# The place of weight splits in the tails of a two-layer hybrid decoder: ahead of the whole layer norm instead of its last 30 instructions

## The chip, the cores and the metric

The kernel runs on one core of one Trainium2 chip. The metric is device time in microseconds (us) of one execution; below is the better. TensorE (PE) multiplies, VectorE (DVE) and ScalarE (ACT) do the elementwise work, GpSimd (POOL) a few additions, and SyncE (SP) starts the transfers. Each engine takes its instructions in the order in which the program lists them.

## What is computed

The input x has 512 positions of 1024 channels. Layer 0 is a mixer of a short convolution and a gated DeltaNet, layer 1 an HGRN2 recurrence; both end in an output projection. What follows each mixer is the tail, and the tails are what this change is about:

```python
for i in range(DEPTH):
    s = conv_gdn_mixer(...) if i % 2 == 0 else hgrn2_mixer(...)      # its last step: y @ w_out
    x = layer_norm(DEEPNORM_ALPHA * x + s, ln_g[i], ln_b[i])
    gate = jax.nn.sigmoid((x @ w_pl_gate[i]).astype(jnp.float32))
    x = x + ((p[i] @ w_pl[i]).astype(jnp.float32) * gate).astype(x.dtype)
```

Everything is float32. A product of two float32 operands is made of three products on TensorE: each operand is split into a high part in a shorter format and the rest, and high x high, low x high and high x low are added (lines 115 to 117).

## The kernel before, in words

All data lie channel by channel: 128 channels on the partitions, 512 positions along them, so that x is eight tiles `f` of 128 x 512. Weights come in chunks of 128 x 1024 float32 (0.5 MB). For each chunk SP starts the load into `wraw` (line 105), ScalarE casts it into `whi` (line 107) and VectorE subtracts the two into `wlo` (line 108). All three have three buffers. So the cast of a chunk waits until TensorE is done with the chunk three before, and a load waits until the split of the chunk three before is done. Accumulators in PSUM for projections are also three (line 70): a fourth takes the first one's buffer and waits until that has been read.

`tail` (line 911) is called twice, for the even and the odd layer. In order:

- `out_proj` (line 923) multiplies the mixer's output with the chunks of the output weight into `pout`; VectorE adds the scaled residual while it reads the result out into `rr` (line 941), and GpSimd sums the eight tiles into `racc` (line 945). Tiles 0 to 3 are done for all 512 positions, tiles 4 to 7 in two halves of 256 positions (`hf` 0 and 1). In the second half tile 4 is the last.
- `norm_half` (line 962) normalizes a half: the mean `mu` as a matmul with a constant (line 966), VectorE subtracts it from the eight tiles (line 971), ScalarE squares (line 973), VectorE adds up into `qacc` (line 975), the variance `var` by a matmul (line 977), then `ve` (line 979) and three Newton steps for the inverse square root (lines 155 to 159), each of three instructions that need the one before, the product with it (line 983), scale and offset on ScalarE (line 985), and the split of the result into `x1h` and `x1l` (lines 163 and 164). The first half's norm runs beside the second half's output projection, the second half's beside what follows.
- The projection of p, `ppl`: two chunks of w_pl, eight tiles of six matmuls of 512 columns each; ScalarE scales each into `pl` (line 1014).
- The gate, `pgate`: eight chunks of w_pl_gate, eight tiles f, each half 24 matmuls of 256 columns. The first halves of tiles 0, 1 and 2 come first, then, when the second norm is done, their second halves, then the other tiles. Tanh on ScalarE (line 1026), two steps on VectorE (lines 1027 and 1028), and a store.

A scheduler puts the instructions of each engine into order by their priority, which falls along the program as it is written; `norm_half` is fed in between the matmuls of the other work by a list of steps (`pump`, line 125). An offset lifts instructions above those written up to so many places earlier:

```python
with self.tc.high_priority(offset=self.prio):
    nc.scalar.copy(hi, raw)
    nc.vector.tensor_tensor(lo, raw, hi.bitcast(F32), op=SUB)
```

`self.prio` is 0 in the layers. The tail sets it to `PRIO` (line 42) at line 992, ahead of the second halves of the output projection, and back to 0 at its end.

Of the kernel before, what the change touches and what calls it, by code (L numbers as in the profile page):

```python
# [38 lines left out]
LN = 2, 7  # L39
GD = 7, 4, 4, 9, 4, 3  # L40
EO = 'f0 g f1 a0 f2 a1 f3 a2 f4 a3 f5 a4 f6 f7 a5 a6 a7'
PRIO = 30


SM_CA, SM_CB, SM_AL, SM_DT, SM_GN, SM_HN, SM_LN, SM_LB, SM_N = 0, 24, 120, 128, 136, 137, 138, 170, 202
# [2 lines left out]
class K:  # L48
# [862 lines left out]
    def tail(self, layer, wout, last):  # L911
# [5 lines left out]
        with tp(name=f"tail{layer}", bufs=1, reuse_waits="tile") as lp, self.psum(f"pt{layer}") as self.ps:  # L917
# [5 lines left out]
            def out_proj(fs, t0, n, held=None):  # L923

                ts = slice(t0, t0 + n)
                accs = [self.acc("pout")[:, :n] for _ in fs]
                chunks = list(held or [])
                for i in range(2):
                    kh = 1 - i if held else i
                    for j, (f, ps) in enumerate(zip(fs, accs)):  # L930
                        if not held or i:
                            chunks.append(self.chunk(wout[2 * f + kh], 16 if n == S else 32))
                        hi, lo = chunks[-1 if not held or i else j]
                        for k in range(8):
                            self.mm3(ps, [(hi[:, k, :], lo[:, k, :], self.yh[kh * 8 + k][:, ts],
                                           self.yl[kh * 8 + k][:, ts])], i == 0 and k == 0, i == 1 and k == 7)
                            self.pump(n / S)
                for f, ps in zip(fs, accs):
                    xr = lp.tile([P, S], F32, tag="xr", name="xr", bufs=2)[:, :n]
                    nc.sync.dma_start(xr, xsrc[:, f * S + t0:f * S + t0 + n])  # L940
                    nc.vector.scalar_tensor_tensor(rr[f][:, ts], xr, ALPHA, ps, op0=MUL, op1=ADD)
                    for hf in range(t0 // HT, (t0 + n) // HT):
                        hs = slice(hf * HT, (hf + 1) * HT)
                        if f:
                            nc.gpsimd.tensor_tensor(racc[hf], rr[0][:, hs] if f == 1 else racc[hf],
                                                    rr[f][:, hs], op=ADD)
                return chunks[-len(fs):]
# [5 lines left out]
            def load_p():  # L953
                praw = self.wp.tile([P, 2 * S], F32, tag="wraw", name="praw", bufs=3)
                nc.sync.dma_start(praw, a["pT"][layer])
                self.split_to(ph.rearrange("p a b -> p (a b)"), pl_.rearrange("p a b -> p (a b)"), praw)
# [34 lines left out]
            held = out_proj((5, 6, 7), 0, HT)  # L991
            self.prio = PRIO
            load_p()
# [134 lines left out]
```

## Time and profile before

| | us |
|---|---|
| median of 3 runs (1216.73 to 1220.0) | 1218.28 |
| the profiled execution | 1218.49 |
| its span, first to last instruction | 1216.8 |
| TensorE busy in it | 1198.5 |
| VectorE, ScalarE, GpSimd busy | 805.7, 563.4, 46.1 |

The even tail stands at about 478 to 627 us of the span, the odd one at 1086 us to its end. Times in the rows are us from the start of the span. A timeline row gives start, length, engine, line, operation, what it writes and reads, and in brackets how long the engine was idle before and what ended that. A matmul's length goes from its issue to the modelled end of its passage, so lengths overlap and the distance between starts is the pace. Where equal instructions follow each other, one row gives them all (x4).

### The profile page before, as it was taken

The numbers are of one execution on the slowest core, as the hardware profiler recorded it, in microseconds if no ns is written. First come the engines' busy times: TensorE is split into PE (matmuls) and PEld (weight loads), VectorE is DVE, ScalarE is ACT, GpSimd is POOL, SyncE is SP. The second block draws the span as 40 slices with busy tenths as digits, with TensorE's granted clock in tenths as the row PEclk, the third lists the DMA queues.
The fourth block names the chain that finished last, engine by engine and source line by source line (L and its number), as shares of the span: only waits on it lengthen the run. The fifth ranks groups of instructions, "written<-read, shape, count | busy, mean of one in ns | idle before, by whom it ended". The sixth has DMA issues, their size and how long they took to land.

```text
span 1216.8 us, 23689 instructions
## 1 busy us (share of the span) xinstructions
PE 1198.5 (98%) x9590; PEld 1020.4 (84%) x9590; DVE 805.7 (66%) x1835; ACT 563.4 (46%) x1340; POOL 46.1 (4%) x75
## 2 busy tenths in 40 slices
PE   7999999999999999999999999999999999999998
PEld 5777878777788788898998888888888888889988
DVE  7778767776768755349856575665657575744884
ACT  5554645454545443127633444444544444433471
POOL 4000000000000000111000000000000000001100
PEclk9999999999999999999999999999999999999999
DMA  6223222222223123353442222222122222234422
GB/s 213 91 79 94 69 88 88 70 90 85 87 71 97 61 70 104 126 161 120 141 148 81 77 88 70 88 69 90 53 87 88 70 88 70 88 104 152 143 92 100
DMA packets 37310, 117.08 MB, mean 96 GB/s; under 512 B 4144, under 2 KB 8016, under 8 KB 37200
## 3 DMA queue, kind: packets, MB, share of 16 engines
q1 hardware_dynamic: 37200, 115.56, 29.5%
q8 instruction: 75, 1.23, 0.4%
q14 instruction: 35, 0.29, 0.1%
HBM read 111.32 MB, written 4.23 MB: 95 GB/s over the span
## 4 chain that ended last, share of the span: by engine, by line
PE 84%; DVE 8%; ACT 4%; DMA 1%; issue 1%; POOL 0%; SPq 0%; DVEq 0%; ACTq 0%; POOLq 0%
PE pz L115 5%; PE pz L117 5%; PE pz L116 5%; PE pout L115 4%; PE pout L117 4%; PE pout L116 4%; PE pqkv L116 3%; PE pqkv L117 3%; PE pqkv L115 3%; PE pf L115 3%; PE pf L117 2%; PE pf L116 2%; PE pq L115 2%; PE pq L117 2%; PE pq L116 2%; PE pgate L116 2%
## 5 line engine op out<-in xcount | busy, mean ns | idle before, releaser
L107 ACT CAST whi<-wraw 128x1024 fp32r<-128x1024 f32 (+1 forms) x196 | 200.4, 1022 | 333.1 <-PE pout L116 86.6
L108 DVE TENSOR_TENSOR wlo<-wraw,whi 128x1024 fp32r<-128x1024 f32 (+1 forms) x196 | 238.3, 1216 | 161.7 <-ACT whi L107 156.8
L115 PE MATMUL pout<-yh,whi 128*128 128x256 f32 (+1 forms) x384 | 122.3, 319 | 0.0
L117 PE MATMUL pout<-yh,wlo 128*128 128x256 f32 (+1 forms) x384 | 122.1, 318 | 0.0
L116 PE MATMUL pout<-yl,whi 128*128 128x256 f32 (+1 forms) x384 | 121.7, 317 | 0.0
L115 PE MATMUL pz<-xh,whi 128*128 128x512 f32 x256 | 103.7, 405 | 0.2 <-DVE scr L413 0.2
L117 PE MATMUL pz<-xh,wlo 128*128 128x512 f32 x256 | 100.6, 393 | 0.0
L116 PE MATMUL pz<-xl,whi 128*128 128x512 f32 x256 | 100.3, 392 | 0.0
L115 PE MATMUL pqkv<-xh,whi 128*128 128x512 f32 x192 | 78.9, 411 | 5.0 <-ACT xh L163 5.0
L117 PE MATMUL pqkv<-xh,wlo 128*128 128x512 f32 x192 | 77.2, 402 | 2.3 <-DVE wlo L108 2.3
L116 PE MATMUL pqkv<-xl,whi 128*128 128x512 f32 x192 | 78.0, 406 | 0.0
L116 PEld LDWEIGHTS pout<-yl,whi 128*128 128x128 f32 x384 | 72.9, 190 | 5.0
L115 PEld LDWEIGHTS pout<-yh,whi 128*128 128x128 f32 x384 | 72.2, 188 | 5.1
L117 PEld LDWEIGHTS pout<-yh,wlo 128*128 128x128 f32 x384 | 72.3, 188 | 5.0
L115 PE MATMUL pi<-whi,xh 128*128 128x256 f32 x256 | 72.7, 284 | 0.0
L116 PE MATMUL pi<-wlo,xh 128*128 128x256 f32 x256 | 72.1, 282 | 0.0
L116 PE MATMUL pgate<-x1l,whi 128*128 128x256 f32 x256 | 71.2, 281 | 0.4 <-DVE x1l L164 0.4
L117 PE MATMUL pi<-whi,xl 128*128 128x256 f32 x256 | 71.2, 278 | 0.0
L117 PE MATMUL pgate<-x1h,wlo 128*128 128x256 f32 x256 | 70.8, 279 | 0.0
L115 PE MATMUL pgate<-x1h,whi 128*128 128x256 f32 x256 | 70.7, 281 | 0.0
L117 PEld LDWEIGHTS pz<-xh,wlo 128*128 128x128 f32 x256 | 48.1, 188 | 10.2
L115 PEld LDWEIGHTS pz<-xh,whi 128*128 128x128 f32 x256 | 48.1, 188 | 9.9 <-issue 0.6
(326 smaller groups left out, 2865.5 us busy)
## 6 DMA issues: line engine op xcount, KB each, us to landing
wraw<-in_we SPq DMA_DIRECT2D x62, 512.0 KB, 3.5
wraw<-in_wo SPq DMA_DIRECT2D x48, 512.0 KB, 3.5
wraw<-in_woe SPq DMA_DIRECT2D x21, 512.0 KB, 3.5
wraw<-in_woo SPq DMA_DIRECT2D x21, 512.0 KB, 3.5
wraw<-in_wg SPq DMA_DIRECT2D x16, 512.0 KB, 3.6
wraw<-in_wi SPq DMA_DIRECT2D x16, 512.0 KB, 3.4
gb<-drows SPq DMA_DIRECT2D x8, 512.0 KB, 3.7
xraw<-in_xT SPq DMA_DIRECT2D x8, 256.0 KB, 4.4
```

The costliest lines, as they stand in the source:

```text
L107: nc.scalar.copy(hi, raw)
L108: nc.vector.tensor_tensor(lo, raw, hi.bitcast(F32), op=SUB)
L115: nc.tensor.matmul(ps, wh, xh, start=first and i == 0, stop=False)
L116: nc.tensor.matmul(ps, wh, xl, start=False, stop=False)
L117: nc.tensor.matmul(ps, wl, xh, start=False, stop=last and i == n - 1)
```

## The change

One number is another. The offset of the splits in the tails goes from 30 to 600 places, so that the scheduler puts a split ahead of the whole layer norm, as soon as its place in the program allows, and not only ahead of the 30 instructions that were written before it. Loads, buffers, tiles and arithmetic stay as they are.

```diff
@@ -39,7 +39,7 @@
 LN = 2, 7
 GD = 7, 4, 4, 9, 4, 3
 EO = 'f0 g f1 a0 f2 a1 f3 a2 f4 a3 f5 a4 f6 f7 a5 a6 a7'
-PRIO = 30
+PRIO = 600
```

The same difference appears in both tails. In the names below (the even tail) a number at the end tells tiles of one name apart: `wlo_6302`, `wlo_6345` and `wlo_6375` are splits of the last three chunks of the output weight, `wlo_6429` and `wlo_6506` those of the two chunks of w_pl, `wlo_6595`, `wlo_6626` and `wlo_6657` those of the first three chunks of w_pl_gate. A leading - is the place before, + the place now.

VectorE, at the end of the first half's sums of squares:

```order
+L108 TENSOR_TENSOR wlo_6302<-wraw_6300,whi_6301 128x1024 [waits DMAHW4_49,PE_49,Activation_49]
 L975 TENSOR_TENSOR qacc_6104<-qacc_6104,sq_6129 128x256 [waits DVE_49,Activation_49]
 L975 TENSOR_TENSOR qacc_6104<-qacc_6104,sq_6133 128x256 [waits DVE_49,Activation_49]
-L108 TENSOR_TENSOR wlo_6302<-wraw_6300,whi_6301 128x1024 [waits DMAHW4_49,PE_49,Activation_49]
+L941 SCALAR_TENSOR_TENSOR rr5_5534<-xr_6330,pout_6083 128x256 [waits DMAHW5_49,PE_49]
 L979 TENSOR_SCALAR ve_6179<-var_6103 128x256 [waits PE_49]
+L108 TENSOR_TENSOR wlo_6345<-wraw_6343,whi_6344 128x1024 [waits DMAHW7_49,Activation_49]
```

The split of a chunk now stands ahead of the last two sums, and the next split between `ve` and the inverse square root; the evacuation of tile 5 has come ahead of `ve`.

VectorE, at the end of the first half's norm, around the evacuation of the second half's last tile (`rr4`, from `pout_6342`):

```order
+L108 TENSOR_TENSOR wlo_6595<-wraw_6593,whi_6594 128x1024 [waits DMAHW5_49,PE_49,Activation_49]
 L164 TENSOR_TENSOR x1l0_2_6072<-rr2_5531,x1h0_2_6071 128x256 [waits Activation_49]
 L164 TENSOR_TENSOR x1l0_3_6074<-rr3_5532,x1h0_3_6073 128x256 [waits Activation_49]
 L164 TENSOR_TENSOR x1l0_4_6076<-rr4_5533,x1h0_4_6075 128x256 [waits Activation_49]
+L983 TENSOR_TENSOR rr7_5536<-rr7_5536,lny_6181 128x256 [waits DVE_49]
+L941 SCALAR_TENSOR_TENSOR rr4_5533<-xr_6403,pout_6342 128x256 [waits DMAHW4_49]
 L164 TENSOR_TENSOR x1l0_5_6078<-rr5_5534,x1h0_5_6077 128x256 [waits Activation_49]
-L941 SCALAR_TENSOR_TENSOR rr4_5533<-xr_6403,pout_6342 128x256 [waits DMAHW4_49,PE_49]
```

The split of the first chunk of w_pl_gate was 16 places behind `rr4` and is now five ahead of it; that of the second chunk of w_pl was eight behind and is now 12 ahead, among the products of line 983, and that of the first chunk of w_pl, which stood five ahead, is now inside the Newton steps.

TensorE, in the projection of p; `ppl_6486` is its third tile:

```order
 L116 MATMUL ppl_6442<-pl_5540,whi_6428 128x512
 L117 MATMUL ppl_6442<-ph_5539,wlo_6429 128x512
-L966 MATMUL mu_6449<-racc1_5538,onesD_220 128x256 [waits Pool_49]
 L115 MATMUL ppl_6486<-ph_5539,whi_6428 128x512 [waits DVE_49]
 L116 MATMUL ppl_6486<-pl_5540,whi_6428 128x512
+L966 MATMUL mu_6449<-racc1_5538,onesD_220 128x256 [waits Pool_49]
```

The mean of the second half has gone two matmuls back. The variance of the second half moves on TensorE from behind the ninth gate matmul to behind the first, and on VectorE the split `wlo_6657` from ahead of its `ve` to behind it. After the norm two gate chunks' casts go ahead of the first two tanh. On ScalarE a cast moves with each split.

## Rows read from the trace of the kernel before

**Rows 1.** The page: busy us (share of the span) and instructions of each engine.

```profile
PE 1198.5 (98%) x9590; PEld 1020.4 (84%) x9590; DVE 805.7 (66%) x1835; ACT 563.4 (46%) x1340; POOL 46.1 (4%) x75
```

**Rows 2.** TensorE's waits in the tails: us in total, times, longest.

```profile
PE ppl L117 <- DVE wlo L108: 1.9, 2, 1.2
...
PE pgate L116 <- DVE x1l L164: 0.4, 2, 0.2
```

**Rows 3.** Timeline of TensorE, even tail: start, length, instruction, idle before.

```profile
554.94 0.67 PE L977 MATMUL var<-qacc,onesD 128*128 128x256 f32 x2
...
568.29 0.39 PE L115 MATMUL ppl<-ph,whi 128*128 128x512 f32 x1
...
569.64 0.50 PE L117 MATMUL ppl<-ph,wlo 128*128 128x512 f32 x1 [0.72 <-DVE wlo L108]
...
572.20 0.70 PE L966 MATMUL mu<-racc,onesD 128*128 128x256 f32 x2
...
581.04 0.28 PE L115 MATMUL pgate<-x1h,whi 128*128 128x256 f32 x1
...
590.22 0.29 PE L115 MATMUL pgate<-x1h,whi 128*128 128x256 f32 x1
590.71 0.38 PE L116 MATMUL pgate<-x1l,whi 128*128 128x256 f32 x1 [0.20 <-DVE x1l L164]
```

**Rows 4.** Timeline of TensorE, odd tail.

```profile
1154.06 0.40 PE L115 MATMUL ppl<-ph,whi 128*128 128x512 f32 x1
...
1155.84 0.50 PE L117 MATMUL ppl<-ph,wlo 128*128 128x512 f32 x1 [1.15 <-DVE wlo L108]
...
1176.28 0.39 PE L115 MATMUL pgate<-x1h,whi 128*128 128x256 f32 x1
1176.87 0.39 PE L116 MATMUL pgate<-x1l,whi 128*128 128x256 f32 x1 [0.20 <-DVE x1l L164]
```

**Rows 5.** Busy us of each engine in two stretches, even tail; PEclk, DMA share, GB/s.

```profile
550.00:560.00 10.00, 10.00 (x85) 9.94 (x84) 9.77 (x19) 4.61 (x7) 0.85 (x1) 1.00 0.53 161
560.00:570.00 10.00, 9.28 (x76) 8.79 (x75) 9.87 (x22) 6.63 (x14) 1.57 (x2) 1.00 0.39 130
```

**Rows 6.** Timeline of GpSimd: the last addition of the even tail.

```profile
571.40 0.74 POOL L945 TENSOR_TENSOR racc<-racc,rr 128x256 f32<-128x256 f32 x1 [6.25 <-DVE rr L941]
```

**Rows 7.** Timeline of VectorE, even tail.

```profile
554.81 1.23 DVE L108 TENSOR_TENSOR wlo<-wraw,whi 128x1024 fp32r<-128x1024 f32 x1
555.95 0.42 DVE L979 TENSOR_SCALAR ve<-var 128x256 f32<-128x256 f32 x1
...
568.37 1.21 DVE L108 TENSOR_TENSOR wlo<-wraw,whi 128x1024 fp32r<-128x1024 f32 x1
569.51 1.42 DVE L164 TENSOR_TENSOR x1l<-rr,x1h 128x256 fp32r<-128x256 f32 x4
570.85 0.41 DVE L941 SCALAR_TENSOR_TENSOR rr<-xr,pout 128x256 f32<-128x256 f32 x1
...
583.30 0.42 DVE L979 TENSOR_SCALAR ve<-var 128x256 f32<-128x256 f32 x1
```

**Rows 8.** Timeline of ScalarE: the cast for the split at 554.81 us.

```profile
553.73 1.05 ACT L107 CAST whi<-wraw 128x1024 fp32r<-128x1024 f32 x1 [0.42 <-PE pout L116]
```

**Rows 9.** Timeline of VectorE, odd tail: the evacuation of `rr4`.

```profile
1157.05 0.41 DVE L941 SCALAR_TENSOR_TENSOR rr<-xr,pout 128x256 f32<-128x256 f32 x1
```

**Rows 10.** Timeline of TensorE: its longest wait after the start.

```profile
21.65 0.50 PE L117 MATMUL pqkv<-xh,wlo 128*128 128x512 f32 x1 [2.33 <-DVE wlo L108]
```

**Rows 11.** Stretches as in rows 5: start of the kernel, after that wait, the end.

```profile
5.00:10.20 5.20, 5.18 (x12) 3.79 (x13) 3.74 (x7) 3.36 (x8) 0.92 (x2) 1.00 0.97 333
...
21.70:26.00 4.30, 4.30 (x19) 3.57 (x20) 4.25 (x11) 1.58 (x2) 0.00 (x0) 1.00 0.59 181
...
1212.70:1215.20 2.50, 0.00 (x0) 0.00 (x0) 0.85 (x2) 0.37 (x1) 0.00 (x0) 1.00 0.13 48
1215.40:1216.80 1.40, 0.00 (x0) 0.00 (x0) 0.00 (x0) 0.00 (x0) 0.00 (x0) 0.50 0.00 0
```

## The prediction

> **What bounds the kernel now.** I read the page's busy shares first, then TensorE's waits, then the timelines of TensorE, VectorE and ScalarE in the two stretches that the table touches (about 547 to 600 us in the tail of the even layer, 1133 to 1186 us in that of the odd one). TensorE is busy for 1198.5 of 1216.8 us [rows 1], so a change to splits can only give back what TensorE still waits for. In the tails that is little [rows 2]: two waits of the projection of p (`ppl`) for a VectorE split, 1.9 us together, and two of the gate for `x1l`, 0.4 us together. Seen in the starts, where the matmuls before and after a wait tell what it cost, the first `ppl` chunk lost 0.89 us in the even tail (three 512-column matmuls at 0.23 us from 568.29 would put the third at 568.75; it starts at 569.64) and 1.3 us in the odd tail (1154.52 against 1155.84) [rows 3, 4]. The gate, whose matmuls start 0.12 us apart, lost 0.4 us between 590.22 and 590.71 and, with a late start of the one before, 0.6 us up to 1176.87. **The most that the change can give is thus some 3.2 us of 1218, 0.26%.** 0.3%, or 3.65 us, is about what a measurement of this kernel can tell from no change.
>
> What can be lost is decided on VectorE. From 550 to 570 us it is busy for 19.6 of 20 us [rows 5], so whatever is put ahead of another instruction there pushes it back by its whole length. Three later steps hang on its order: the evacuation of the last output projection (`rr4`, line 941, 570.85 us), the mean `mu` of the second half, which TensorE computes after GpSimd has added that evacuation [rows 6], and the second half's `x1l`.
>
> **The change, part by part.** The number of instructions, their shapes and their DMAs stay as they are; GpSimd's order is the same, SP's moves one weight load ahead of two stores. Only places move.
>
> *The first `wpl` split.* Its VectorE part moves from 568.37 us [rows 7] into the inverse square root, to about 564.3. TensorE wants it at 568.75. The waits of 0.89 and 1.3 us at the third `ppl` matmul go.
>
> *What the split runs into: the variance of the first half is later.* The split before it starts at 554.81 us [rows 7] and can't come sooner, since its ScalarE cast is released by TensorE, at 553.73 [rows 8]. Before, all sums of squares were done by then and `ve` began at 555.95. Now two sums stand behind the split: 554.81 + 1.14 = 555.95, the second at 556.40, done at 556.82; then `var` on TensorE, 0.67 [rows 3], and two semaphores: `ve` at 557.60, **1.65 us late**.
>
> *What now stands ahead of `rr4`.* From `ve` to `rr4` VectorE took 570.85 - 555.95 = 14.90 us. Two more splits stand in that stretch (the second `wpl` chunk and the first gate chunk), 2 x 1.14 = 2.28, the pace from 568.37 to 569.51 [rows 7]. Two instructions leave it (the evacuation of `rr5`, now ahead of `ve`, and one `x1l`), 2 x 0.34 = 0.68, the pace of the four instructions from 569.51 to 570.85. In the inverse square root, where a dependent step starts 0.45 and an independent one 0.33 us after the one before, splits and evacuations now stand in more of the gaps; adding the paces up one by one in the new order gives 0.67 less. So `rr4` comes 1.65 + 2.28 - 0.68 - 0.67 = **2.58 us later**, at 573.4. The casts of these splits are ready by then: the gate chunk's waits for TensorE's last `pout` matmul, one place ahead of the row at 568.29, and for three steps of the norm on ScalarE; it is done near 570.4 by my estimate, and VectorE reaches its part near 570.9.
>
> *Who waits.* The accumulators of line 70 are three, so the third `ppl` tile takes the buffer that `rr4` evacuates: TensorE can't begin its 13th `ppl` matmul before. It gets there at 568.29 + 12 x 0.23 = 571.05 and is released at 573.4 + 0.42 + 0.05 = 573.9: a new wait of 2.85 us. `mu` follows two matmuls later; it came 1.35 us after `rr4` began (572.20 - 570.85), so now at 574.78, with another 0.4 us of waiting. Against `mu` at 572.20 [rows 3] that is + 2.58; two `ppl` matmuls that stood behind it are now ahead, - 0.46: the first gate matmul moves from 581.04 to **583.16, + 2.12 us**.
>
> *The second half's norm.* Its last sum now waits for ScalarE's scaling of the seventh `ppl` tile, so `ve` comes about 1.05 us after the first gate matmul (2.26 before: 583.30 - 581.04), but the third gate chunk's split, 1.14, now stands between `ve` and the inverse square root. 1.05 + 1.14 = 2.19: `x1l` keeps its place against the gate within 0.07, and so does the wait of 0.4 us there. The gain from there on is nothing, and nothing is lost: the two gate casts that now go ahead of the tanh cost 2 x 1.05 on ScalarE while TensorE still has the 24 matmuls of the third gate product, 24 x 0.12 = 2.9 us, before it needs what they release.
>
> *Sum.* + 2.12 - 0.07 = + 2.05 us in the even tail. The odd tail repeats it: `rr4` starts at 1157.05 [rows 9], 586.2 later, as do the split and `ve` ahead of it, while TensorE comes to `ppl` 0.4 us sooner. Its wait is longer (3.3 us), but the end of it, `mu` and the gate move by the same amount. Together **+ 4.1 us**. On the profiled execution's own 1218.49 us (span 1216.8 and 1.7 around it) that is 1222.6; that execution stands 0.2 over the median of 1218.28, so **1222.4 us, + 0.34%**.
>
> *Bounds of what no row shows.* How much of the splits fits into gaps of VectorE is worked out, not read. If `ve` is not late at all, `rr4` moves by 0.93 and the sum is 2 x (0.93 - 0.46 - 0.07) = + 0.8 us. If no gap is filled and the delay of `ve` grows by another half, + 2 x (0.67 + 0.8) more: + 7.0. I take the middle since the row at 554.81 fixes the start of the stretch and the rows from 568.37 to 570.85 its pace.
>
> **Rivals.** *The clock falls in the new wait.* TensorE sat idle for 2.33 us before 21.65 [rows 10] and the granted clock was 1.00 after it; after the last matmul it was 1.00 for the next 2.5 us and 0.50, the lower level of 1.2 GHz, from 1215.40 on [rows 11]. The new waits, 2.85 and 3.3 us with another 0.4 close behind, are longer than the one that did no harm and about as long as the one that did. At the start, from 5.0 to 10.2 us, 12 matmuls of 512 columns took 5.2 us, 0.43 each, against 0.23 later; the price of one fall, by that row, is 12 x 0.20 = 2.4 us. It decides from about 2.6 us of idleness. One fall gives 1218.28 + 4.1 + 2.4 = 1224.8, two 1227.2. For it: the waits are in that range in both tails; against it: the waits are broken by two matmuls.
>
> The Trainium skill ("TensorE: Matmul & The Clock Gate", section "Part 1: The HAM clock gate") says that TensorE's clock falls to its lower level after an idle stretch, and (section "HAM oscillation — how this bites in real kernels") that a long wait before each group of matmuls makes each group start slow. The end of this trace agrees that it falls; that a wait inside the work does it, no row here shows. By that rule the time would be that of this rival.
>
> *VectorE takes it up, and the kernel is not slower.* If `rr4` moves by less than 0.53 us (0.46 for the two matmuls ahead of `mu` and 0.07), the removed waits count alone. The mechanism: the sums and the Newton steps leave 0.1 us gaps, ScalarE waits less between its casts, and both fill up. The price is then at best that of all waits, - 3.2, and for half of them - 1.6: 1216.7. Against it: two whole splits, 2.28 us, stand ahead of `rr4`, and the stretch had no idle time.
>
> *Only the splits count.* `ve` is on time and the sum is the lower bound: + 0.8, 1219.1.
>
> **How the numbers follow.** Forecast as summed (1220.5 to 1224): 0.42. Clock: 0.25. Only the splits (1218.5 to 1220.5): 0.20. Not slower: 0.13. Slower by over 0.3% is above 1221.93: two thirds of the forecast (0.28) and the clock, 0.53. Faster by over 0.3% is below 1214.63, more than all waits are worth: 0.02. The rest, 0.45, is within 0.3%. The range leaves out most of the case that isn't slower (0.12) and two clock falls (0.06): 1218.0 to 1226.0.
>
> **What would show it.** In the profile after, TensorE's waits should have `ppl` L115 behind `rr4` L941 with 2 to 3.5 us in each tail, and no longer `ppl` L117 behind a split; `ve` of the first half 2.8 us after the third split's start, not 1.14; `rr4` behind two more splits; GpSimd's last addition and `mu` some 2.6 us later; the first gate matmul 2 us later against the first `ppl` matmul plus its old wait. Matmuls near 0.43 us after the wait would be the clock. `rr4` less than a microsecond late would break the walk along VectorE; a late `rr4` with TensorE on time would break the claim that the accumulator holds it.

## The result, and the profile after

The changed kernel takes 1227.98 us (median of 6 runs, 1226.79 to 1229.02) against 1218.76 us of the kernel before (6 runs): the ratio is 1.0078, with a 95% interval of 1.0068 to 1.0088. It is **slower by 0.78%**, 9.2 us. The forecast was 1222.4 us with a range of 1218 to 1226: the direction was right, the time lies 2 us outside the range.

The page first (busy us, share of the span, instructions), then TensorE's waits (us in total, times, longest).

```profile
span 1226.8 us, 23700 instructions
PE 1205.1 (98%) x9590; PEld 1024.4 (84%) x9590; DVE 804.0 (66%) x1835; ACT 563.6 (46%) x1340; POOL 46.3 (4%) x75
```

```profile
PE ppl L115 <- DVE rr L941: 5.7, 2, 3.1
...
PE pgate L116 <- DVE x1l L164: 0.2, 1, 0.2
```

The span grew by 10.0 us while TensorE, with the same 9590 matmuls, became *busier* by 6.6 us [rows 1]. So waits alone can't be it: the matmuls themselves have become longer. The two waits of `ppl` for the split [rows 2] are gone, and in their place stand two for the evacuation `rr` of line 941.

TensorE's timeline in the even tail shows both (start, length, instruction, idle before).

```profile
567.52 0.40 PE L115 MATMUL ppl<-ph,whi 128*128 128x512 f32 x1
...
570.04 0.39 PE L117 MATMUL ppl<-ph,wlo 128*128 128x512 f32 x1
573.48 0.79 PE L115 MATMUL ppl<-ph,whi 128*128 128x512 f32 x1 [3.06 <-DVE rr L941]
574.08 0.63 PE L116 MATMUL ppl<-pl,whi 128*128 128x512 f32 x1
574.74 1.22 PE L966 MATMUL mu<-racc,onesD 128*128 128x256 f32 x2
...
576.62 0.63 PE L116 MATMUL ppl<-pl,whi 128*128 128x512 f32 x1
577.04 0.63 PE L117 MATMUL ppl<-ph,wlo 128*128 128x512 f32 x1
...
579.99 0.39 PE L115 MATMUL ppl<-ph,whi 128*128 128x512 f32 x1
580.22 0.39 PE L116 MATMUL ppl<-pl,whi 128*128 128x512 f32 x1
...
585.46 0.28 PE L115 MATMUL pgate<-x1h,whi 128*128 128x256 f32 x1
```

The twelve matmuls up to 570.04 start 0.23 us apart. Then comes the wait, and behind it the starts are 0.43 us apart (576.62 to 577.04) until 579.99, where the pace is 0.23 again. The granted clock says the same (stretch, its length, PE busy and matmuls, PEclk, DMA share, GB/s): 1.00 through most of the idle time, then 0.50, the level of 1.2 GHz. It fell inside the wait, just before the matmul at 573.48.

```profile
571.00:573.00 2.00, 0.00 (x0) 1.00 0.46 125
573.00:574.00 1.00, 0.52 (x1) 0.55 0.64 221
574.00:579.00 5.00, 4.96 (x12) 0.50 0.12 50
...
580.00:581.00 1.00, 1.00 (x6) 1.00 0.00 0
```

The odd tail repeats it with a wait of 2.65 us; its clock is 0.50 as well.

```profile
1158.28 0.40 PE L115 MATMUL ppl<-ph,whi 128*128 128x512 f32 x1
...
1163.84 0.79 PE L115 MATMUL ppl<-ph,whi 128*128 128x512 f32 x1 [2.65 <-DVE rr L941]
...
1175.90 0.28 PE L115 MATMUL pgate<-x1h,whi 128*128 128x256 f32 x1
```

```profile
1164.00:1170.00 6.00, 5.96 (x14) 0.50 0.17 70
```

One yardstick serves for all runs below: **from the first `ppl` matmul to the first gate matmul**. Before it was 12.75 us in the even tail (581.04 - 568.29, [rows 3]) and 13.16 in the odd one (1167.22 - 1154.06). Now it is 17.94 and 17.62: + 5.19 and + 4.46, together 9.65 us. The stretches outside it differ too, by 0.8 to 1.3 us either way, and nearly cancel: that is why 9.65 comes so close to the 10.0 of the span.

VectorE's timeline shows why `rr4` is late; its instructions answer to [rows 7].

```profile
554.16 1.23 DVE L108 TENSOR_TENSOR wlo<-wraw,whi 128x1024 fp32r<-128x1024 f32 x1 [0.62 <-ACT whi L107]
555.31 0.95 DVE L975 TENSOR_TENSOR qacc<-qacc,sq 128x256 f32<-128x256 f32 x2
556.17 0.41 DVE L941 SCALAR_TENSOR_TENSOR rr<-xr,pout 128x256 f32<-128x256 f32 x1
557.05 0.42 DVE L979 TENSOR_SCALAR ve<-var 128x256 f32<-128x256 f32 x1 [0.46 <-PE var L977]
...
570.54 1.21 DVE L108 TENSOR_TENSOR wlo<-wraw,whi 128x1024 fp32r<-128x1024 f32 x1
...
573.02 0.41 DVE L941 SCALAR_TENSOR_TENSOR rr<-xr,pout 128x256 f32<-128x256 f32 x1
```

Two sums stand behind the split at 554.16, `ve` comes 2.89 us after that split (1.14 before), and `rr4` 18.86 us after it (16.04 before).

### The profile page after: what moved, and what is told of

Read it like the earlier page. It is cut to its first block, busy times and chain, and to the rows that moved or that the text cites. A ratio compares the mean times of both kernels' runs of the same rounds, so it can differ in the third digit from the quotient of the medians.

```text
span 1226.8 us, 23700 instructions
## 1 busy us (share of the span) xinstructions
PE 1205.1 (98%) x9590; PEld 1024.4 (84%) x9590; DVE 804.0 (66%) x1835; ACT 563.6 (46%) x1340; POOL 46.3 (4%) x75
## 4 chain that ended last, share of the span: by engine, by line
PE 87%; DVE 8%; ACT 2%; issue 1%; DMA 1%; POOL 0%; SPq 0%; DVEq 0%; POOLq 0%
PE pz L115 5%; PE pz L117 5%; PE pz L116 5%; PE pout L115 4%; PE pout L116 4%; PE pout L117 4%; PE pqkv L116 3%; PE pqkv L117 3%; PE pqkv L115 3%; PE pf L115 2%; PE pf L117 2%; PE pf L116 2%; PE pq L116 2%; PE pq L117 2%; PE pq L115 2%; PE pgate L116 2%
```

## The experiments

In the table at the end of this section, "clock low" is how long the granted clock was 0.50 in that tail, all in all; it is worked out as twice the sum of (1 - granted clock) x 0.5 us over half-microsecond windows.

### Is it the clock? (e2, e7, e8, e11)

e2 is the changed kernel with work for TensorE while `rr4` is late:

```
-                pl = []
+                pl, dump = [], self.pg("dump")
...
-                        self.pump(2)
+                        [nc.tensor.matmul(dump, hi[:, 2, :], ph[:, 0, :], start=True, stop=True) for _ in range(17 * (cix == 0 and j == 1))]; self.pump(2)
```

> The changed kernel with 17 matmuls of 512 columns that nobody reads (17 x 0.23 = 3.9 us), put on TensorE behind the second ppl tile, so that it has work while rr4 is late; they add nothing to the result. The mean now stands ahead of the third ppl tile. Theory (half of the loss is the wait, the larger half the clock that falls in it): the granted clock is 1.00 in both tails, the ppl matmuls behind keep their 0.23 us, and the time falls by 2 x (3.1 - 0.46) = 5.3 us to about 1222.7 us although TensorE got work added. Rival (the wait is the whole loss and the low clock is in the record without costing time): 1228 us or, with the fillers' work, more.

Measured 1223.44 us (ratio to before 1.0040, interval 1.0028 to 1.0053). TensorE's timeline, and the windows:

```profile
570.55 4.01 PE L1012 MATMUL dump<-ph,whi 128*128 128x512 f32 x17
574.64 0.70 PE L966 MATMUL mu<-racc,onesD 128*128 128x256 f32 x2
```

```profile
570.00:575.00 5.00, 4.93 (x24) 1.00 0.52 187
575.00:580.00 5.00, 5.00 (x24) 1.00 0.01 3
```

The mean comes as late as in the changed kernel (6.84 us after the first `ppl` matmul, 7.22 there), yet 34 added matmuls make the kernel 4.5 us *faster*. Some 0.9 us of that is the mean's new place ahead of two `ppl` matmuls (0.46 in each tail, by the expectation); the rest is the clock. It costs time by itself: some 4 of the 9.2 us are not the wait.

e7 and e8 are e2 with 9 and with 6 such matmuls (`range(9 * ...)`, `range(6 * ...)`), so that part of the wait is idle again.

> As e2 with 9 matmuls that nobody reads in place of 17, so that TensorE has work for 2.1 us of the 4.1 and is idle for about 2.0 us at the mean. The mean comes at the same time as in e2. Theory (the wait costs by the clock too as soon as the clock falls in it, and e3 fell with waits of 1.58 and 0.52 us): the clock falls for some 3.4 us in each tail and the time is 1226 us. Rival (it takes 2.6 us of idleness, as the prediction had it): clock 1.00, 1223.4 us as e2.

> As e2 with 6 matmuls that nobody reads: idle for about 1.7 us ahead of the third ppl tile and 0.5 us ahead of the mean, which stands two matmuls behind it again. 0.46 us less in each tail than e2 by that order. Theory (these waits are those of e3, in which the clock fell): a fall in each tail, 1225 us. Rival (2.6 us of idleness are needed): clock 1.00, 1222.5 us.

e7: 1223.15 us (ratio 1.0041, 1.0027 to 1.0055). e8: 1223.94 us (1.0047, 1.0033 to 1.0061). In both profiles the clock stayed at 1.00 in both tails; here a wait of e7 and one of e8:

```profile
575.69 0.70 PE L966 MATMUL mu<-racc,onesD 128*128 128x256 f32 x2 [1.87 <-POOL racc L945]
```

```profile
1160.53 0.50 PE L115 MATMUL ppl<-ph,whi 128*128 128x512 f32 x1 [1.70 <-DVE rr L941]
```

My theory, that a fall comes with any such wait, fell; the rival held for these lengths. e8 has the order of the changed kernel at the mean, so it comes nearest to **the late `rr4` without the clock**: 15.10 and 15.51 us from `ppl` to the gate, + 2.35 in each tail. The forecast had + 2.12. Its median is 4.0 us under the changed kernel's.

e11 is the changed kernel once more, one execution.

> The changed kernel once more, unaltered, for a second profile. In e4 the same even tail with a wait of 3.05 us lost half as much clock as in the first profile (the clock 0.50 for 3.4 us, not 6.4). Theory (what a wait costs in clock is not fixed by its length alone and differs between executions): waits of 3.1 and 2.7 us again, the low stretch in at least one tail of another length than 6.4 us; 1225 to 1229 us. Rival (it is fixed by the program): 6.4 us at 0.50 in both tails, 1228 us.

Measured 1228.19 us, with waits of 3.06 and 3.05 us; the clock was low for 3.4 us in each tail, half as long as the 6.8 us of the first profile (the expectation's 6.4 is the same stretch, read more coarsely):

```profile
574.00:575.00 1.00, 0.00 (x0) 1.00 0.54 66
575.00:578.00 3.00, 2.93 (x6) 0.51 0.38 153
578.00:579.00 1.00, 1.00 (x4) 0.76 0.00 0
```

So the same wait doesn't always cost the same. Counted from the third `ppl` tile's first matmul to the gate, which leaves the wait itself out, e8 took 9.54 and 9.55 us, the changed kernel 11.98 and 12.06 in the first profile and 10.57 and 10.98 in the second: a fall cost **2.4 and 2.5 us there, 1.0 and 1.4 here**. The total is the same for another reason: in e11 the clock fell a third time, near the start of the kernel, behind the wait of TensorE that stands there in every kernel of this record ([rows 10] in the kernel before). It was low for 3.4 us:

```profile
22.28 0.80 PE L117 MATMUL pqkv<-xh,wlo 128*128 128x512 f32 x1 [2.53 <-DVE wlo L108]
```

```profile
22.50:25.50 3.00, 3.00 (x8) 0.50 0.71 193
```

By an estimate from these rows that is 8 matmuls, each 0.20 us slower than at 1.00, 1.6 us; e11 reached the even `ppl` at 569.06 us, 1.54 later than the first profile (567.52), while both gates took the same to 0.01 us.

**The wait at the start is a test of its own**, since no edit touches that part of the program. In nine of the 13 profiles it is 2.53 to 2.59 us long; behind it the clock fell in six (e3, e4, e5, e6, e7, e11) and stayed up in three (after, e9, e10). In the other four, the kernel before among them, it is 1.62 to 2.33 us long and the clock stayed up.

### One part at a time (e3, e4)

e4 leaves the odd tail as before:

```
-            self.prio = PRIO
+            self.prio = 30 if last else PRIO
```

> 600 in the tail of the even layer alone, 30 in that of the odd one. Theory (each tail pays its own wait and its own fall of the clock, 2.1 + 3.1 us): half of the loss, 1223.5 us, the clock 0.50 once, near 574 us. Rival (one tail makes most of it, or the even one's loss is taken up again by the odd layer): 1219 or 1227 us.

1223.43 us (ratio 1.0038, 1.0026 to 1.0050): half of the loss, and `ppl` to gate 17.09 us in the even tail, 12.74 in the odd one. Each tail pays for itself. The odd tail has the order of before here and took 0.4 us less than in the profile of before (13.16): so much the yardstick varies from one execution to the next.

e3 leaves the gate chunks as before:

```
                 for f in range(KD):
+                    self.prio = 30
                     ch = self.chunk(a["wg"][layer * KD + f], 32)
```

> 600 for the splits of the output projection and of w_pl, 30 for those of the gate chunks, so that one split less stands ahead of rr4. Theory: rr4 comes 1.5 us sooner than in the changed kernel (571.5 in the even tail), TensorE waits about 1.6 us for it instead of 3.06, the clock stays up since 2.33 us did no harm elsewhere, the gate starts 1 us later than before in each tail: 1220.4 us. Rival a (any wait there brings the clock down): 1.0 + 3.1 in each tail, 1226.7 us. Rival b (the gate chunks' splits don't matter): 1228 us with waits of 3 us.

1222.72 us (ratio 1.0033, 1.0020 to 1.0046). The even tail:

```profile
574.47 0.50 PE L115 MATMUL ppl<-ph,whi 128*128 128x512 f32 x1 [1.58 <-DVE rr L941]
...
575.72 0.70 PE L966 MATMUL mu<-racc,onesD 128*128 128x256 f32 x2 [0.52 <-POOL racc L945]
```

```profile
576.00:577.00 1.00, 1.00 (x4) 0.65 0.00 0
577.00:579.00 2.00, 2.00 (x6) 0.50 0.00 0
```

The wait for `rr4` is 1.58 us, as expected; so the first gate chunk's split made up half of it. But here the clock fell, after a wait that the prediction held to be harmless, in the even tail (15.85 us from `ppl` to gate, + 3.10). In the odd one, with waits of 1.19 and 0.53, it did not (14.02, + 0.86: the wait without the clock, about the 1.0 expected). Between the theory and its rival a, one tail each.

### Is it `rr4` alone? (e1, e5)

e1 puts `rr4` ahead of the splits:

```
-                    nc.vector.scalar_tensor_tensor(rr[f][:, ts], xr, ALPHA, ps, op0=MUL, op1=ADD)
+                    with self.tc.high_priority(offset=1200 if f == 4 and t0 else 0): nc.vector.scalar_tensor_tensor(rr[f][:, ts], xr, ALPHA, ps, op0=MUL, op1=ADD)
```

> The changed kernel with one more priority: the evacuation of the second half's last tile (rr4, line 941) goes four places up on VectorE, ahead of the products of line 983 and of the first gate chunk's split. All splits stay in front of the norm, as in the change. Theory (the loss is TensorE's wait for rr4 and the fall of its clock behind that wait): rr4 starts near 569.5 us instead of 573.0, the third ppl tile waits no more, the mean has a wait of 0.6 us in place of the 3.06, no matmul takes 0.43 us in the tails, and the time is 1217.5 us, 0.9% under the changed kernel and within 0.2% of before. Rival (the splits in front of the norm cost by themselves, since they make the norm and all behind it late): the clock may stay up, but the gate starts late all the same; 1222 us or more.

A miss: 1233.78 us (ratio 1.0123, 1.0109 to 1.0137), slower than the changed kernel. The time is within the rival's bound, but neither text had what holds TensorE here. `rr4` did come early (1.62 us after the first `ppl` matmul, 5.50 in the changed kernel), and the wait for it is gone. TensorE waits for other things instead:

```profile
PE mu L966 <- POOL racc L945: 6.9, 2, 3.6
...
PE ppl L115 <- ACT pl L1014: 4.6, 2, 2.3
```

GpSimd's addition of `rr4`, 0.74 us before [rows 6], is the cause of the first; GpSimd's row and two of VectorE:

```profile
570.67 3.92 POOL L945 TENSOR_TENSOR racc<-racc,rr 128x256 f32<-128x256 f32 x1 [5.62 <-DVE rr L941]
```

```profile
573.26 0.75 DVE L983 TENSOR_TENSOR rr<-rr,lny 128x256 f32<-128x256 f32 x2
575.91 0.42 DVE L971 TENSOR_TENSOR rr<-rr,mu 128x256 f32<-128x256 f32 x1 [1.90 <-PE mu L966]
```

VectorE works without a gap until 574.01, and the addition ends at 574.59, 0.58 us later. It is the same wherever it begins: in e6 (below) it starts at 572.89, VectorE stops at 574.09, it ends at 574.67; in the changed kernel 573.57, 574.10, 574.69. Before, it began in a gap of VectorE of 0.43 us (up to 571.69) and took 0.74. The Trainium skill ("SBUF — State Buffer", section "SBUF: two separate sides") says that VectorE and GpSimd share a pair of SBUF ports, which a VectorE instruction with two SBUF inputs can hold against GpSimd for as long as it runs. The traces agree, and say more: eight VectorE instructions in a row, not one, kept the addition waiting. It goes the other way round as well. In the changed kernel the addition before this one got in at once, and VectorE's split beside it took 1.76 us in place of 1.2 (GpSimd's row, VectorE's row):

```profile
563.68 0.79 POOL L945 TENSOR_TENSOR racc<-racc,rr 128x256 f32<-128x256 f32 x1 [2.69 <-DVE rr L941]
```

```profile
563.79 1.76 DVE L108 TENSOR_TENSOR wlo<-wraw,whi 128x1024 fp32r<-128x1024 f32 x1
```

e5 tests what the addition on GpSimd costs by doing it on VectorE, with the priority of `rr4` (the lines that extend that priority to it are left out):

```
-                            nc.gpsimd.tensor_tensor(racc[hf], rr[0][:, hs] if f == 1 else racc[hf],
+                            (nc.vector if f == 4 and t0 else nc.gpsimd).tensor_tensor(racc[hf], rr[0][:, hs] if f == 1 else racc[hf],
```

> As e1 (rr4 four places up on VectorE), with one more edit: the last addition into the sum of the second half (line 945, rr4 onto racc) runs on VectorE behind rr4 and not on GpSimd, where it took 3.92 us in e1 against 0.74 before. Theory (GpSimd was kept off SBUF while VectorE ran products, x1l and a split without a gap; the mean then waited for it): the addition takes 0.42 us, the mean is ready near 571.3 us, its wait of 3.25 and 3.6 us goes. The wait of 2.3 us for the evacuation of a ppl tile by ScalarE, which stands behind a cast, stays. Without any fall of the clock 1218.9 - 2.2 (the two waits for the split) + 2 x 2.3 = 1221.3 us; with one short fall in each tail some 3 us more. Rival (GpSimd's length is only its own late start, the mean is held by the late norm): little is gained, 1231 us or more.

1222.82 us (ratio 1.0038, 1.0026 to 1.0050), 11 us less than e1 (10 by the two ratios). In VectorE's and TensorE's timelines the addition takes 0.41 us, and the mean comes 2.76 us after the first `ppl` matmul at 569.72, where it was 6.15 in e1:

```profile
572.01 0.41 DVE L945 TENSOR_TENSOR racc<-racc,rr 128x256 f32<-128x256 f32 x1
```

```profile
572.48 0.70 PE L967 MATMUL mu<-racc,onesD 128*128 128x256 f32 x2
...
579.85 0.80 PE L115 MATMUL ppl<-ph,whi 128*128 128x512 f32 x1 [2.55 <-ACT pl L1015]
```

What is left is the second wait of e1: ScalarE's evacuations of the `ppl` tiles now stand behind squares, a cast and steps of the norm, and TensorE runs out of accumulators. In the even tail the clock fell behind that wait of 2.55 us, in the odd one behind one of 2.54 it did not.

### Is there a version that keeps the gain? (e6, e9, e10)

e6 moves one split only, in the kernel before:

```
-                    hi, lo = self.chunk(a["wpl"][layer * 2 + cix])
+                    self.prio = PRIO if cix else 600; hi, lo = self.chunk(a["wpl"][layer * 2 + cix]); self.prio = PRIO
```

> The kernel before, with 600 for the first w_pl chunk's split alone and 30 for all others. Theory (the change was right on one split, and wrong since the splits behind it came along): TensorE's wait of 0.72 and 1.15 us for that split goes, rr4 stays within half a microsecond of its place, no new wait over 1 us, clock 1.00: 1218.9 - 2.2 = 1216.7 us. Rival (the norm, now with a split between its products, makes rr4 or x1l late enough to eat it): 1219 us or more.

1222.06 us (ratio 1.0033, 1.0021 to 1.0046); the theory fell. TensorE gets through the first two tiles 0.89 us sooner and then stands at the mean. GpSimd and TensorE:

```profile
572.89 1.78 POOL L945 TENSOR_TENSOR racc<-racc,rr 128x256 f32<-128x256 f32 x1 [6.44 <-DVE rr L941]
```

```profile
574.73 0.70 PE L966 MATMUL mu<-racc,onesD 128*128 128x256 f32 x2 [2.66 <-POOL racc L945]
```

Of the 2.66 us some 0.9 is the old wait, moved one step on; 0.6 is `rr4` (3.18 us after the first `ppl` matmul, 2.56 before) and 1.0 the addition of 1.78 us. The odd tail had the same 2.66 us, and its clock stayed up; in the even one it was low for 3.4 us, and near the start of the kernel for another 3.4.

e9 joins what e1, e3 and e5 left over (600 up to `w_pl`, 30 for the gate chunks, `rr4` first, its addition on VectorE): its edits are those three together. e10 has the edits of e1, e5 and e6.

> What the runs so far leave over, put together: 600 for the splits of the output projection and of w_pl as in e3 (both waits for a split go), 30 for the gate chunks (no cast ahead of ScalarE's evacuations, the block of 2.5 us of e5), rr4 up on VectorE as in e1, its addition on VectorE as in e5. Theory (the change's own aim is worth the two waits for a split, once rr4, the addition and ScalarE are kept clear): TensorE waits about 0.4 us for the mean and for nothing longer in the tails, clock 1.00: 1218.5 - 2.2 to 1218.5 - 3.2, some 1216 us, 0.2% faster than before. Rival (the norm is late behind the splits whatever is done for rr4, and x1l or the second norm takes it back): 1218.5 us or more.

> e6 (only the first w_pl chunk's split at 600) with rr4 up on VectorE and its addition there. Theory: the 2.66 us at the mean of e6, of which 1.0 was GpSimd's longer addition (1.78 against 0.74) and the rest rr4 behind products, falls under 1.2 us, clock 1.00, 1217 to 1218 us. Rival (the norm's start with the split in it is what costs): 1221 us or more.

e9: 1220.81 us (ratio 1.0022, 1.0013 to 1.0031), no fall of the clock, but a wait of 1.5 us in each tail for ScalarE's evacuation of a `ppl` tile and 14.13 us to the gate: the rival's time came. What takes the gain back is ScalarE, whose evacuations stand behind steps of the first norm and squares of the second; `x1l`, which the rival also named, is not waited for. e10: 1216.94 us (ratio 0.9990, 0.9982 to 0.9999), a tenth of a per cent faster than before and the fastest here; its theory (1217 to 1218 us, no wait over 1.2 us, clock 1.00) held. Its longest waits in the tails:

```profile
PE mu L967 <- DVE racc L945: 1.1, 2, 0.7
...
PE pgate L116 <- DVE x1l L164: 0.4, 2, 0.2
```

That isn't the gain sought, though: from `ppl` to the gate it takes 12.85 and 13.29 us, no less than before. What its profile has ahead of before, it has in the pace of the gate's matmuls (last section), and that this comes from the edit is not shown.

| run | tail | waits in `ppl` and at the mean, us | clock low, us | `ppl` to gate, us |
|---|---|---|---|---|
| before | even / odd | 0.72 / 1.15 | 0 / 0 | 12.75 / 13.16 |
| e1 | even / odd | 3.25 + 2.32 / 3.64 + 2.32 | 3.4 / 3.4 + 3.4 | 19.68 / 21.64 |
| after | even / odd | 3.06 / 2.65 | 6.8 / 6.8 | 17.94 / 17.62 |
| e11 (after again) | even / odd | 3.06 / 3.05 + 0.52 | 3.4 / 3.4 | 16.54 / 16.95 |
| e4 | even / odd | 3.05 + 0.52 / 0.72 | 3.4 / 0 | 17.09 / 12.74 |
| e6 | even / odd | 2.66 / 2.66 | 3.4 / 0 | 16.34 / 14.75 |
| e5 | even / odd | 2.55 / 2.54 | 3.4 / 0 | 16.34 / 15.05 |
| e2 | even / odd | 0 / 0.47 | 0 / 0 | 16.03 / 16.42 |
| e7 | even / odd | 1.87 / 2.27 | 0 / 0 | 16.04 / 16.44 |
| e8 | even / odd | 1.29 + 0.52 / 1.70 + 0.52 | 0 / 0 | 15.10 / 15.51 |
| e3 | even / odd | 1.58 + 0.52 / 1.19 + 0.53 | 3.4 / 0 | 15.85 / 14.02 |
| e9 | even / odd | 0.24 + 1.48 / 0.24 + 1.49 | 0 / 0 | 14.13 / 14.12 |
| e10 | even / odd | 0.32 + 0.16 / 0.75 | 0 / 0 | 12.85 / 13.29 |

Each of e1's tails has two long waits; in the odd one the clock fell behind both, the second of 2.32 us. Read as shares, wait by wait and with the waits at the start of the kernel: over 3 us the clock fell six times of six; between 2.5 and 2.7 us three times of five in the tails and six of nine at the start; between 1.8 and 2.4 us once in seven; between 1.1 and 1.8 us once in eight (e3, where another wait of 0.52 us stands two matmuls behind).

## Why the prediction was wrong, point by point

**Right: what bounds the kernel, and the walk along VectorE.** The most to be gained was put at 3.2 us, and no version got more. The waits for the split went. `ve` came 2.89 us after the third split (forecast 2.79); `rr4` moved by 18.86 - 16.04 = 2.82 us against that split (forecast 2.58). That the third `ppl` tile is held by `rr4`'s accumulator is the row of 5.7 us; the wait was to be 2.85 us in the even tail and was 3.06 (3.21 from start to start, which is how the forecast counted). In the odd tail 3.3 was forecast and 2.65 came, since TensorE reached `ppl` later in that execution; in e11 it was 3.05. The second half's norm kept its place against the gate: one wait of 0.2 us for `x1l` is left.

**Right, a little small: the sum without the clock.** + 2.12 us to the gate was forecast; e8 shows + 2.35 in each tail. Two tails make 4.7 us where the sum had 4.1, a difference within what one tail varies.

**Wrong: that the clock would stay up.** This is the step that failed. The sum has nothing for it; measured, it is 4.95 us of 9.65 in the first profile and 4.0 of 9.2 us by the median of e8. The clock rival named the mechanism and the place, and its time for two falls, 1227.2 us, is close to the 1227.98 measured. It got a chance of 0.25, and two falls 0.06, which the range left out. Three things were wrong with that. The rival's own point of decision, "about 2.6 us of idleness", lay *below* both waits that the same text had worked out (2.85 and 3.3), so by its own numbers two falls were the likeliest case; and what was set against it, that the waits are broken by two matmuls, spoke only of the 0.4 us behind them, not of the unbroken wait ahead. The one row of a harmless wait, 2.33 us [rows 10], was too short to speak for 2.85, and it was one execution: at 2.53 to 2.59 us the same wait brought the clock down in six profiles of nine. No fixed length decides it either, as "about 2.6 us" has it: 2.66 us did no harm in e6's odd tail, 2.32 did in e1's. The Trainium skill's rules cited there ("TensorE: Matmul & The Clock Gate", sections "Part 1: The HAM clock gate" and "HAM oscillation — how this bites in real kernels") pointed the right way. These traces agree with them inside the work too, not only at the end: after the idle stretches of 3.06 and 2.65 us the matmuls of `ppl` started 0.43 us apart.

**Luck: the price of a fall.** The forecast's 2.4 us is 12 matmuls too slow by 0.20 us, read off the start of the kernel; but the granted clock in that row is 1.00 [rows 11], so the row doesn't show that a fall made them slow, nor how long one lasts. The first profile's 2.4 and 2.5 us agree with it, the 1.0 and 1.4 of e11 don't.

The sum as measured, by the yardstick: 4.7 us for the waits (2.75 and 1.95, what the clock's 2.44 and 2.51 leave of 5.19 and 4.46) and 4.95 us for the clock, 9.65 together.

**The 0.4 us at the mean** that the sum had as a wait is not in the first profile: with the clock at half, the two matmuls ahead of `mu` took so long that it was ready. In e11's odd tail and in e4, where the clock fell later, it stands there with 0.52 us.

**The other rivals** (VectorE takes it up; only the splits count) needed `rr4` to move by less than 0.53 or by 0.93 us. At 2.82 neither was near.

**Not seen at all: GpSimd.** The prediction let `mu` follow `rr4` by a fixed 1.35 us. In the changed kernel that did little harm (the addition took 1.12 us instead of 0.74), but it is 1.0 of the 2.66 us that TensorE waits in e6, and the first of the two waits that made e1 the slowest. It isn't all: e5, with the addition on VectorE, still lost 5 us to ScalarE's evacuations and the clock.

## What to carry to other kernels

Where a bound engine can be made to wait, add up the longest unbroken wait that the change makes and treat the clock as part of the price from the length at which a fall has been seen, not as a side case: here a new wait of 3 us in place of one of about 1 cost 2.35 us a tail, and the clock up to another 2.5. One trace in which a wait did no harm is no evidence that it does none; look at the same wait in other executions. An offset that moves a whole class of instructions also moves those that nobody needs yet, past the one (`rr4`) that somebody does. Even the one split that TensorE needed early was not worth moving here: alone it uncovered a longer wait (e6), and with that wait cleared away the tail took as long as before (e10). And before work on GpSimd is put on the path, look at whether VectorE has gaps while it runs.

## What was not expected of the hardware

GpSimd's 128 x 256 addition of 0.74 us took 1.12, 1.78 and 3.92 us, and ended 0.58 us after VectorE's run of instructions without a gap was over, however early it began; the engine of that one addition was worth 11 us between e1 and e5 (in part through the clock and the order behind it).

The same program's waits of 3.06 us were followed by 6.8 us at 0.50 in one execution and 3.4 us in another, and two tails of one execution with the same wait (2.66 us in e6) differed in whether the clock fell. So did the wait at the start of the kernel, in a part of the program that no edit touched. What decides that is left open.

Matmuls of 256 columns go at one of two paces at a granted clock of 1.00: taken over 32 of them at a time, 0.113 or 0.118 us from start to start. Twelve us late in the odd gate, in e10 and in e8 (columns as above; the number of matmuls is in brackets):

```profile
1198.00:1210.00 12.00, 12.00 (x109) 1.00 0.18 67
```

```profile
1204.00:1216.00 12.00, 12.00 (x104) 1.00 0.17 67
```

Over a whole gate stage, from its first to its last matmul, that is 44.48 us (1166.30 to 1210.78) in e10 against 46.46 (1170.08 to 1216.54) in e8, 2 us of 45, and before it was 46.36 in the even and 45.16 in the odd tail. It is why stretches, and not totals of single profiles, are set against each other here. What sets the pace was not tried.
